# Transposing the residual for five RMS norms: TensorE transposes replaced by VectorE squares and 32-partition DMAs on ScalarE's queue

## The chip, the cores and the metric

The kernel runs on one core of a Trainium2 chip. The metric is the device time of one execution in microseconds. One more execution is taken by the hardware profiler, and its records are the trace that is read here. The engines are called as the profile calls them: PE is TensorE's matmul side and PEld its weight loads, DVE is VectorE, ACT is ScalarE, POOL is GpSimd, and SPq is the queue of SyncE, which issues DMAs.

## The reference

Two decoder layers act on a residual `h` of 256 tokens by 2048 channels in float32. Cut to what matters here:

```python
for i in range(2):
    hn = rms_norm(h, ln_mix_w[i])
    h = h + (even_mixer, odd_mixer)[i](hn, ...)          # ends with  @ w_out  (2048 x 2048)
    hn = rms_norm(h, ln_mlp_w[i])
    h = h + square(relu(hn @ w_up[i])) @ w_down[i]       # 2048 x 8192 and 8192 x 2048
    hn = rms_norm(h, ln_ple_w[i])
    h = h + sigmoid(hn @ w_ple_gate[i]) * (p[i] @ w_ple_proj[i])
return rms_norm(h, ln_final_w)
```

Six of the seven norms feed a matmul, so six times the residual is needed with its channels on the partitions. The last norm only scales rows.

## The kernel before

**Layout.** `h` lies in SBUF as 128 partitions by 2 token tiles by 2048 channels: tokens on the partitions. A matmul with `h` wants the channels on the partitions. So a `Norm` object turns `h` block by block; a block is 512 channels, and a norm has 4 of them. The turned and scaled residual goes into an `XT`: for each group of 128 channels (a k-tile, 16 in all) a high part, rounded to the format `fp32r`, and a low part, the rest. The scale by the root mean square is applied later; `stats` sums the squares of a block on ACT (the operand is called `junk`).

**Weights.** `split_w` loads a chunk (two k-tiles by 512 columns, 512 KB) with a DMA on SP's queue into `wraw` (4 buffers). ACT writes its high part `whi` (L198), then DVE the low part `wlo` (L199); each has 3 buffers. So a chunk costs one ACT cast and one DVE subtraction, and ACT can cast a chunk when PE is done with the chunk three earlier. A product of two float32 numbers is three matmuls: high by high, high by low, low by high.

**Projections.** `project` takes a chunk in 12 matmuls of 512 columns; `project_wide`, which `w_up` and layer 1's input projection use, in 16 matmuls of 512 or 256 columns. Eight chunks make one projection (`nb`) of 512 output columns. At the end of a projection `nb` of `out_proj`, of the last quarter of `w_down`, and of `ple`, `h` gets its new 512 columns, and `close` starts the norm's block for them.

**Order of the work.** A block is a generator. It waits in the lane "tail" of `Background`, and the next projection advances it by one step at each tick, once or twice per chunk. For the last block of a norm `close` drains the lane at once, so all of that block's instructions stand ahead of the next projection in program order. A scheduler may shift instructions a little within an engine. Each engine then works in program order, and an instruction that waits holds up all behind it.

**A block before.** PE transposes 8 squares of 128 x 128 into two PSUM banks (L175); from there ACT writes the high parts (L224) and DVE the low parts (L225), 4 instructions each of 256 columns.

**Semaphores of DMAs.** All DMAs of all queues count on eight semaphores (DMAHW0 to DMAHW7), which are given out in turn. A DMA on a semaphore starts only when the DMA that had it before has landed.

Of the kernel before, what the change touches and what calls it, by code (L numbers as in the profile page):

```python
# [10 lines left out]
F32 = mybir.dt.float32  # L11
# [6 lines left out]
D = 2048  # L18
# [107 lines left out]
def pause(n):  # L126

    for _ in range(n):
        yield
# [3 lines left out]
def trunk_kernel(ctx, tc, a, out):  # L133
# [68 lines left out]
    class XT:  # L202
# [11 lines left out]
        def put(self, k, n, src, scale=None):  # L214
            o = k % 4
            g = self.group(k // 4)
            w, l = g[:, o:o + n, 0, :], g[:, o:o + n, 1, :]
            if len(src.shape) == 2:
                w, l = g[:, o, 0, :], g[:, o, 1, :]
            if scale is None:  # L220
                nc.scalar.copy(out=w, in_=src)
                nc.vector.tensor_tensor(out=l, in0=src, in1=w, op=ALU.subtract)
            else:
                nc.scalar.activation(out=w, in_=src, func=AF.Copy, scale=scale)  # L224
                nc.vector.scalar_tensor_tensor(  # L225
                    out=l, in0=src, scalar=scale, in1=w, op0=ALU.mult, op1=ALU.subtract
                )
# [23 lines left out]
        nc.tensor.matmul(out=ps[t], lhsT=xh, rhs=wl, start=False, stop=False)  # L251
        nc.tensor.matmul(out=ps[t], lhsT=xl, rhs=wh, start=False, stop=last)  # L252

    def project(ps, xt, kts, w, col, ncol=NB, row_of=None):

        n = len(kts)
        for c, m, (wh, wl) in chunks(kts, row_of or list(kts), w, col, ncol):
            for j in range(m):
                for t in range(NT):
                    multiply(ps, xt, kts[c + j], t, wh[:, j, :], wl[:, j, :], c + j == 0, c + j == n - 1)  # L260
                bg.tick(rates)
# [52 lines left out]
    def add_halves(dst, ps, pool):  # L314
        s = pool.tile([P, T], F32, tag="half", name="half", bufs=2)
        nc.scalar.copy(out=s, in_=ps[:, T:2 * T])  # L316
        nc.vector.tensor_add(out=dst, in0=ps[:, 0:T], in1=s)  # L317

    def acc_pair():
        return [atile() for _ in range(NT)]  # L320


    class Norm:


        def __init__(self, which, layer):
            self.which, self.layer = which, layer
            self.xt = XT()
            self.ss = spool.tile([P, NT, 4], F32, tag="ss", name="ss")
            self.cols = None  # L330

        def stats(self, b, ts=range(NT)):
            for t in ts:
# [2 lines left out]
                    out=junk, in_=h[:, t, b * NB:(b + 1) * NB], func=AF.Square, accum_out=self.ss[:, t, b:b + 1]  # L336
                )

        def block(self, b):
            for k in range(4 * b, 4 * b + 4, 2):  # L340
                ps = mtile()
                for j in range(2):
                    for t in range(NT):
                        transpose(ps[:, j * T + t * P:j * T + (t + 1) * P], h[:, t, (k + j) * P:(k + j + 1) * P])
                yield
                for j in range(2):
                    v, c = (vec1, 32 * self.which - 32) if self.which else (vec0, 0)
                    c += 16 * self.layer + k + j
                    self.xt.put(k + j, 1, ps[:, j * T:(j + 1) * T], v[:, c:c + 1])
            yield  # L350
            self.stats(b)
            yield
# [12 lines left out]
    class FinalNorm(Norm):  # L365


        def __init__(self, lnf):
            self.ss = spool.tile([P, NT, 4], F32, tag="ss", name="ss")
            self.lnf = lnf  # L370

        def scale(self, t, b):
            o = h[:, t, b * NB:(b + 1) * NB]
# [65 lines left out]
    def close(norm, b):  # L439

        bg.drain("tail")
        bg.add("tail", norm.block(b))
        if b == 3:
            bg.drain("tail")

    def out_proj(yt, w, kts, norm):
# [9 lines left out]
    def mlp(layer, norm, after):  # L456
        ms = norm.mean_square()
        r2 = spool.tile([P, NT], F32, tag="r2", name="r2")
        nc.vector.reciprocal(out=r2, in_=ms)
        with tc.tile_pool(name="uT", bufs=6) as upool, tc.tile_pool(name="u", bufs=3) as up:  # L460
            for fb in range(4):
                ut = XT(upool)
                for nb in range(4):
                    ps = project_wide(norm.xt, range(KT), a["w_up"][layer], fb * 2048 + nb * NB)
                    for f in range(4):
                        u = up.tile([P, T], F32, tag="u", name="u")
                        add_halves(u, ps[f], up)
# [24 lines left out]
    def ple(layer, norm, after, pT, pp):  # L492
        rs = norm.rstd()
        for nb in range(4):
# [9 lines left out]
            if end:  # L504
                with tc.tile_pool(name="last", bufs=4) as last:
                    project_apart(ps, norm.xt, a["w_ple_gate"][layer], nb * NB, last)
            else:
                project(ps, norm.xt, range(KT), a["w_ple_gate"][layer], nb * NB)
            for t in range(NT):
                g = pp.tile([P, NB], F32, tag="gate", name="gate", bufs=2)  # L510
                nc.scalar.activation(out=g, in_=ps[t], func=AF.Sigmoid, scale=rs[:, t:t + 1])  # L511
# [9 lines left out]
    def even_mixer(norm, after):  # L521
# [3 lines left out]
        with ExitStack() as st:  # L525
# [6 lines left out]
            def first_rows(c):  # L532

                if c % 4 == 0:
                    bg.drain("tail")
                    load_x(c // 4)
                    gen = norm.block(c // 4)
                    for _ in range(3):
                        next(gen)
                    bg.add("stats", gen)  # L540
                    if c == 12:
                        load_vectors()
                        rates["stats"] = 1
# [471 lines left out]
            for blk in range(2):  # L1015
                channels(Z0 + blk * NB, z_tile(blk))
            bg.drain("tail")
            out_proj(yt, a["ev_w_out"][0], list(range(8, 16)) + list(range(8)), after)


    def odd_mixer(norm, after):
        w_in = a["od_w_in"][0]
        xt = norm.xt
        with ExitStack() as st:
# [8 lines left out]
            yt = XT()  # L1033

            def channels(col, dst, then=None):
                ps = project_wide(xt, range(KT), w_in, col)
                bg.drain("tail")
                if not rows:
                    rows[0] = row_rstd(rs, big)
# [124 lines left out]
            for b in range(2):  # L1164
# [9 lines left out]

                channels(5120 + b * NB, gt, finish)
            bg.drain("tail")
            out_proj(yt, a["od_w_out"][0], range(KT), after)


# [39 lines left out]
    for layer in range(2):  # L1219
        mix, after = (even_mixer, odd_mixer)[layer], Norm(1, layer)  # L1220
        mix(norm, after)
        with tc.tile_pool(name="ple", bufs=1) as pp:
            pT = load_p(layer, pp)
            gate = Norm(2, layer)
            mlp(layer, after, gate)
            if layer == 0:
                norm = Norm(0, 1)
            else:
                lnf = pp.tile([P, D], F32, name="lnf")
                nc.sync.dma_start(out=lnf, in_=a["ln_final_w"].rearrange("(o d) -> o d", o=1).to_broadcast([P, D]))  # L1230
                norm = FinalNorm(lnf)
            ple(layer, gate, norm, pT, pp)
# [26 lines left out]
```

## Time and profile before

| | |
|---|---|
| median of 3 runs | 2504.76 us (2504.16 to 2504.85) |
| the profiled execution's own time | 2507.46 us |
| its span, first to last instruction | 2505.7 us |
| granted TensorE clock, mean | 0.998 of full speed |
| PE busy | 2482.6 us, 99% |
| PEld, DVE, ACT busy | 2150.6, 1493.3, 1179.2 us |
| DMA of the one hardware queue | 58.7% of the 16 DMA engines |

The profiled execution is 0.1% longer than the median run. Its span leaves 1.8 us of its own time outside.

### The profile page before, as it was taken

How to read it: one execution, taken by the hardware profiler on the slowest of the kernel's cores; microseconds unless marked ns; L12 is line 12 of the kernel's file. 1: busy time of each engine (PE TensorE's matmuls, PEld its weight loads, DVE VectorE, ACT ScalarE, POOL GpSimd, SP SyncE). 2: the span in 40 equal slices, each digit the busy share in tenths (PEclk: the TensorE clock that was granted, in tenths of full speed). 3: DMA queues.
4: the chain of work that ended last, by engine and by line, in shares of the span. 5: the costliest groups of instructions: out<-in, count | busy, mean ns of one | idle time of the engine just before them, and what ended most of it. 6: DMA issues, size and time to landing. Idle time of an engine off the chain costs nothing. (4 is left out here: it accounts for less than half of the span.)

```text
span 2505.7 us, 34856 instructions
## 1 busy us (share of the span) xinstructions
PE 2482.6 (99%) x13699; PEld 2150.6 (86%) x13699; DVE 1493.3 (60%) x2083; ACT 1179.2 (47%) x1610; POOL 24.2 (1%) x62
## 2 busy tenths in 40 slices
PE   8999999999999999999999999999999999999998
PEld 8999998888888888888888888888888888888886
DVE  5777865565565565565565465656556555556555
ACT  5523664544444443445554453554434444445454
POOL 0000000000000000000000000000000000000000
PEclk9999999999999999999999999999999999999999
DMA  6443456665665665665566655666566566566554
GB/s 206 130 124 107 122 168 191 182 191 189 190 192 189 190 190 192 189 190 182 186 214 191 192 151 168 199 184 192 187 192 190 190 192 189 190 193 187 185 189 153
DMA packets 237125, 452.88 MB, mean 181 GB/s; under 512 B 16417, under 2 KB 19361, under 8 KB 236705
## 3 DMA queue, kind: packets, MB, share of 16 engines
q1 hardware_dynamic: 236960, 450.66, 58.7%
q8 instruction: 107, 1.75, 0.3%
q14 instruction: 58, 0.47, 0.0%
HBM read 448.50 MB, written 2.10 MB: 180 GB/s over the span
## 5 line engine op out<-in xcount | busy, mean ns | idle before, releaser
L199 DVE TENSOR_TENSOR wlo<-wraw,whi 128x1024 fp32r<-128x1024 f32 x840 | 1027.1, 1225 | 899.1 <-ACT whi L198 895.0
L198 ACT CAST whi<-wraw 128x1024 fp32r<-128x1024 f32 x840 | 881.9, 1051 | 1192.6 <-PE acc L252 608.3
L303 PE MATMUL acc<-xt,whi 128*128 128x512 f32 x2560 | 806.1, 396 | 0.0
L250 PE MATMUL acc<-whi,xt 128*128 128x512 f32 x1664 | 655.3, 394 | 0.0
L252 PE MATMUL acc<-whi,xt 128*128 128x512 f32 x1664 | 650.8, 391 | 0.0
L251 PE MATMUL acc<-wlo,xt 128*128 128x512 f32 x1664 | 646.9, 389 | 0.0
L307 PEld LDWEIGHTS acc<-xt,wlo 128*128 128x128 f32 x2560 | 480.7, 188 | 113.4
L307 PE MATMUL acc<-xt,wlo 128*128 128x256 f32 x2560 | 503.5, 278 | 0.0
L303 PEld LDWEIGHTS acc<-xt,whi 128*128 128x128 f32 x2560 | 391.0, 189 | 1.2
L252 PEld LDWEIGHTS acc<-whi,xt 128*128 128x128 f32 x1664 | 312.3, 188 | 70.2
L251 PEld LDWEIGHTS acc<-wlo,xt 128*128 128x128 f32 x1664 | 312.5, 188 | 66.7
L250 PEld LDWEIGHTS acc<-whi,xt 128*128 128x128 f32 x1664 | 312.7, 188 | 62.1
L288 PE MATMUL acc<-xt,whi 128*128 128x256 f32 x768 | 224.2, 294 | 2.3 <-ACT whi L198 1.7
L289 PE MATMUL acc<-xt,whi 128*128 128x256 f32 x768 | 219.1, 286 | 0.8 <-DVE xt L225 0.8
L290 PE MATMUL acc<-xt,wlo 128*128 128x256 f32 x768 | 218.6, 286 | 0.8 <-DVE wlo L199 0.8
L288 PEld LDWEIGHTS acc<-xt,whi 128*128 128x128 f32 x768 | 148.4, 194 | 3.5 <-ACT whi L198 2.6
L289 PEld LDWEIGHTS acc<-xt,whi 128*128 128x128 f32 x768 | 149.1, 194 | 1.3 <-DVE xt L225 1.0
L290 PEld LDWEIGHTS acc<-xt,wlo 128*128 128x128 f32 x768 | 148.3, 194 | 1.5 <-DVE wlo L199 1.4
L316 ACT COPY half<-acc 128x256 f32<-128x256 f32 x160 | 59.1, 370 | 40.6 <-DVE u L317 22.8
L225 DVE SCALAR_TENSOR_TENSOR xt<-mps,vec,xt 128x256 fp32r<-128x256 f32 x96 | 43.2, 479 | 16.3 <-ACT xt L224 16.0
L468 DVE SCALAR_TENSOR_TENSOR u<-u 128x256 f32<-128x256 f32 x128 | 51.0, 419 | 0.3
L317 DVE TENSOR_TENSOR u<-acc,half 128x256 f32<-128x256 f32 x128 | 50.8, 417 | 0.0
(270 smaller groups left out, 1078.6 us busy)
## 6 DMA issues: line engine op xcount, KB each, us to landing
wraw<-in_w_up SPq DMA_DIRECT2D x256, 512.0 KB, 3.7
wraw<-in_w_down SPq DMA_DIRECT2D x256, 512.0 KB, 3.7
wraw<-in_ev_w_in SPq DMA_DIRECT2D x96, 512.0 KB, 4.3
wraw<-in_od_w_in SPq DMA_DIRECT2D x96, 512.0 KB, 3.7
wraw<-in_w_ple_gate SPq DMA_DIRECT2D x64, 512.0 KB, 4.3
wraw<-in_ev_w_out SPq DMA_DIRECT2D x32, 512.0 KB, 4.6
wraw<-in_od_w_out SPq DMA_DIRECT2D x32, 512.0 KB, 4.7
wraw<-in_w_ple_proj SPq DMA_DIRECT2D x8, 512.0 KB, 4.5
```

The lines of the kernel that those rows point to most:

```text
L198: nc.scalar.copy(out=w, in_=r)
L199: nc.vector.tensor_tensor(out=l, in0=r, in1=w, op=ALU.subtract)
L250: nc.tensor.matmul(out=ps[t], lhsT=xh, rhs=wh, start=first, stop=False)
L251: nc.tensor.matmul(out=ps[t], lhsT=xh, rhs=wl, start=False, stop=False)
L252: nc.tensor.matmul(out=ps[t], lhsT=xl, rhs=wh, start=False, stop=last)
L288: nc.tensor.matmul(out=ps[f], lhsT=wh[:, j, s], rhs=xt.hi(k), start=first and f % 2 == 0, stop=False)
L289: nc.tensor.matmul(out=ps[f], lhsT=wh[:, j, s], rhs=xt.lo(k), start=False, stop=False)
L290: nc.tensor.matmul(out=ps[f], lhsT=wl[:, j, s], rhs=xt.hi(k), start=False, stop=last and f % 2 == 1)
L303: nc.tensor.matmul(out=ps[f], lhsT=wh[:, j, s], rhs=xt.both(kts[c + j]), start=c + j == 0, stop=False)
L307: nc.tensor.matmul(out=ps[f][:, 0:T], lhsT=wl[:, j, s], rhs=xt.hi(kts[c + j]), start=False, stop=c + j == n - 1)
L316: nc.scalar.copy(out=s, in_=ps[:, T:2 * T])
L468: nc.vector.scalar_tensor_tensor(out=u, in0=u, scalar=0.0, in1=u, op0=ALU.max, op1=ALU.mult)
```

## The change

All norms but the first (which still uses the old block under the name `block_on_pe`) turn a block in another way, 20 blocks in all:

1. One DVE instruction transposes each 32 x 32 square of the block in place of its partition quarter (L362, 128 x 1024).
2. Sixteen DMAs on ACT's queue (L368) move pieces of 32 partitions by 4 runs of 64 numbers (256 bytes) to the partition quarter where they belong, from the tile `turned` to the tile `placed`.
3. `stats` and a pause of four ticks follow. Then come four `put`s, which read `placed` in SBUF: ACT writes 128 x 256 high numbers (L222); the low part is two DVE instructions of 128 x 128 (L224).
4. For a norm's last block `close` runs the first four steps at once and leaves the rest to the ticks; the new hook `whole` drains the lane before chunk 6 of the next projection.

The two tiles share buffers that exist: of the recurrent part in layer 0's mixer, of a query tile in layer 1's, and of the tile `lnf` in `ple`. So the loads of `lnf`, `pin`, `swab` and `retd` come at other places in SP's queue.

```diff
     class Norm:
+        first_steps = 4
         def block(self, b):
+            turned, placed = self.stage()
+            src = h[:, :, b * NB:(b + 1) * NB].rearrange("p t (j c) -> p j t c", c=S)
+            nc.vector.transpose(out=turned, in_=src)
+            yield
+            sq = turned.rearrange("p (k q t r) -> p k q (t r)", q=SB, t=NT, r=S)
+            to = placed.rearrange("p (k i u) -> p k i u", k=4, i=SB)
+            for i in range(SB):
+                for q in range(SB):
+                    nc.scalar.dma_start(out=to[q * S:(q + 1) * S, :, i], in_=sq[i * S:(i + 1) * S, :, q])
+                if i % 2:
+                    yield
+            self.stats(b)
+            yield
+            yield from pause(4)
+            x = placed.rearrange("p (k i t r) -> p k t i r", k=4, i=SB, t=NT)
+            for j in range(4):
+                k = 4 * b + j
+                self.xt.put(k, 1, x[:, j], self.gain(k))
+                yield
+
+        def block_on_pe(self, b):
             for k in range(4 * b, 4 * b + 4, 2):
                 ps = mtile()
...
     def close(norm, b):
         bg.drain("tail")
-        bg.add("tail", norm.block(b))
+        gen = norm.block(b)
         if b == 3:
+            for _ in range(norm.first_steps):
+                next(gen)
+        bg.add("tail", gen)
+
+    def whole(c):
+        if c == KT - 4:
             bg.drain("tail")
...
-                    ps = project_wide(norm.xt, range(KT), a["w_up"][layer], fb * 2048 + nb * NB)
+                    ps = project_wide(norm.xt, range(KT), a["w_up"][layer], fb * 2048 + nb * NB, whole)
...
-                project(ps, norm.xt, range(KT), a["w_ple_gate"][layer], nb * NB)
+                project(ps, norm.xt, range(KT), a["w_ple_gate"][layer], nb * NB, before=whole)
...
+            after.stage = lambda: [lru_tile(n).rearrange("p a t -> p (a t)") for n in ("rr", "ii")]
             out_proj(yt, a["ev_w_out"][0], list(range(8, 16)) + list(range(8)), after)
```

Where the instructions stand, first ACT, at the end of the third projection (`nb` = 2) of layer 1's `out_proj`. Before, from the last cast ahead of the block (names with their buffer numbers, and in brackets the semaphores that an instruction waits for):

```order
L198 CAST whi_14977<-wraw_14976 128x1024 [waits DMAHW2_49,DVE_49,PE_49]
L335 ACTIVATE junk_14972,ss_11888<-h_77 128x512 [waits DVE_49]
L335 ACTIVATE junk_14974,ss_11888<-h_77 128x512 [waits DVE_49,Activation_49]
L224 ACTIVATE xt_14940<-mps_14929,vec1_79 128x256 [waits PE_49]
L198 CAST whi_14995<-wraw_14994 128x1024 [waits DMAHW3_49,DVE_49,PE_49]
```

And of the change at the same place:

```order
L198 CAST whi_15148<-wraw_15147 128x1024 [waits DMAHW0_49,DVE_49,PE_49]
L349 ACTIVATE junk_15143,ss_12023<-h_77 128x512 [waits DVE_49]
L349 ACTIVATE junk_15145,ss_12023<-h_77 128x512 [waits DVE_49,Activation_49]
L368 DMA stage_15101<-stage_15101 32x4x64 [waits DVE_49]
L368 DMA stage_15101<-stage_15101 32x4x64 x3
L368 DMA stage_15101<-stage_15101 32x4x64 [waits DMAHW1_49]
L368 DMA stage_15101<-stage_15101 32x4x64 [waits DMAHW2_49]
L368 DMA stage_15101<-stage_15101 32x4x64 [waits DMAHW3_49]
L368 DMA stage_15101<-stage_15101 32x4x64 [waits DMAHW4_49]
L368 DMA stage_15101<-stage_15101 32x4x64 [waits DMAHW5_49]
L368 DMA stage_15101<-stage_15101 32x4x64 [waits DMAHW6_49]
```

Six more DMAs like these follow, which wait for DMAHW7 and DMAHW0 to DMAHW4, and then the next cast, `whi_15166`. All sixteen DMAs now stand in one row between two casts, where one activation stood. The first waits for the DVE transpose. The fourth has DMAHW0 and the fifth DMAHW1; DMAHW6 goes first to a weight load that SP issues between the second and the third, that of `wraw_15232`. So the tenth DMA waits for that load.

DVE at the same place, before:

```order
L452 TENSOR_TENSOR h_77<-h_77,acc_14744 128x512 [waits PE_49]
L452 TENSOR_TENSOR h_77<-h_77,acc_14745 128x512 [waits PE_49]
L199 TENSOR_TENSOR wlo_14978<-wraw_14976,whi_14977 128x1024 [waits DMAHW2_49,Activation_49]
L225 SCALAR_TENSOR_TENSOR xt_14940<-mps_14929,vec1_79,xt_14940 128x256 [waits Activation_49]
L199 TENSOR_TENSOR wlo_14996<-wraw_14994,whi_14995 128x1024 [waits DMAHW3_49,DVE_49,Activation_49]
```

And of the change:

```order
L500 TENSOR_TENSOR h_77<-h_77,acc_14905 128x512 [waits PE_49]
L362 STREAM_TRANSPOSE stage_15101<-h_77 128x1024 [waits DVE_49]
L199 TENSOR_TENSOR wlo_15149<-wraw_15147,whi_15148 128x1024 [waits DMAHW0_49,Activation_49]
L199 TENSOR_TENSOR wlo_15167<-wraw_15165,whi_15166 128x1024 [waits DMAHW1_49,Activation_49]
L199 TENSOR_TENSOR wlo_15185<-wraw_15183,whi_15184 128x1024 [waits DMAHW2_49,Activation_49]
```

The transpose stands ahead of the subtraction `wlo_15149`. That subtraction frees the buffer into which SP loads `wraw_15232`, so this load starts after the transpose and the subtraction. The same pattern stands in all 20 blocks: in 19 the tenth DMA waits so, in one block of `ple` the eleventh.

SP at the start of layer 1's MLP, before, with the small loads among those of `od_w_out`:

```order
L197 DMA wraw<-in_od_w_out 128x2x512 x7
L484 DMA pin<-in_p 128x2x256
L197 DMA wraw<-in_od_w_out 128x2x512 x3
L1230 DMA lnf<-in_ln_final_w 128x2048
L197 DMA wraw<-in_od_w_out 128x2x512 x22
```

And of the change:

```order
L197 DMA wraw<-in_od_w_out 128x2x512 x32
L197 DMA wraw<-in_w_up 128x2x512 x9
L532 DMA pin<-in_p 128x2x256
L197 DMA wraw<-in_w_up 128x2x512 x23
```

The load of `pin` now stands behind nine loads of `w_up`; PE's four transposes of it stand at the end of that projection's fifth chunk.

## Rows read from the trace of the kernel before

**Rows 1.** The page's busy time of each engine.

```profile
PE 2482.6 (99%) x13699; PEld 2150.6 (86%) x13699; DVE 1493.3 (60%) x2083; ACT 1179.2 (47%) x1610; POOL 24.2 (1%) x62
```

**Rows 2.** Waits: us in total, times, longest us.

```profile
DVE wlo L199 <- ACT whi L198: 895.0, 673, 3.7
ACT whi L198 <- PE acc L252: 608.3, 387, 1.7
```

**Rows 3.** Timeline of PE, end of the third projection of layer 1's out_proj.

```profile
1660.65 0.39 PE L250 MATMUL acc<-whi,xt 128*128 128x512 f32 x1
```

**Rows 4.** Timeline of ACT at the same place: start, us, engine, line.

```profile
1658.13 1.05 ACT L198 CAST whi<-wraw 128x1024 fp32r<-128x1024 f32 x1 [1.67 <-PE acc L252]
1660.85 1.06 ACT L198 CAST whi<-wraw 128x1024 fp32r<-128x1024 f32 x1 [1.67 <-PE acc L252]
...
1663.10 0.18 ACT L335 ACTIVATION_READ_ACCUMULATOR junk<-h 128x1 f32 x1
```

**Rows 5.** Timeline of DVE at the same place.

```profile
1660.36 1.28 DVE L452 TENSOR_TENSOR h<-h,acc 128x512 f32<-128x512 f32 x2
1661.94 1.23 DVE L199 TENSOR_TENSOR wlo<-wraw,whi 128x1024 fp32r<-128x1024 f32 x1 [0.30 <-ACT whi L198]
```

**Rows 6.** Timeline of PE in a block's first half, w_down of layer 1.

```profile
2328.40 0.39 PE L252 MATMUL acc<-whi,xt 128*128 128x512 f32 x1
2328.63 0.60 PE L175 MATMUL mps<-base,h 128*128 128x128 f32 x4
...
2329.30 0.40 PE L251 MATMUL acc<-wlo,xt 128*128 128x512 f32 x1
```

**Rows 7.** Groups by shape: busy us, mean ns of one.

```profile
L778 DVE STREAM_TRANSPOSE dc<-dct 128x128 f32<-128x128 f32 x16 | 4.3, 296 | 0.0
L965 DVE TENSOR_TENSOR ii<-ii,xc 128x1024 f32<-128x1024 f32 x2 | 2.5, 1226 | 6.8 <-ACT ii L960 6.8
```

**Rows 8.** Timeline of SP's queue, DMAs issued one behind the other.

```profile
1.19 0.41 SPq L1193 DMA_DIRECT2D base<-in_c_base  x1
1.65 0.43 SPq L1194 DMA_DIRECT2D h<-in_x  x1
...
38.37 0.46 SPq L616 DMA_DIRECT2D dtb<-in_dn_dt_bias  x1
38.88 0.42 SPq L617 DMA_DIRECT2D alog<-in_dn_a_log  x1
```

**Rows 9.** Tile r, the shortest DMA issue: ns min/median/max.

```profile
L1206 SPq DMA_DIRECT2D r<-in_lru_bx x1: 272/272/272, 16.2 to 16.2; - x1
```

**Rows 10.** The page's DMA issues: median us from issue to landing.

```profile
wraw<-in_w_down SPq DMA_DIRECT2D x256, 512.0 KB, 3.7
wraw<-in_od_w_out SPq DMA_DIRECT2D x32, 512.0 KB, 4.7
```

**Rows 11.** Tile wraw in the stretch 1640 to 1690: landing of its loads.

```profile
DMA to landing us min/median/max: 3.6/4.7/4.9
```

**Rows 12.** Windows: PE busy, PEld, DVE, ACT, POOL, granted clock, DMA share, GB/s.

```profile
24.00:25.00 1.00, 1.00 (x6) 1.00 (x6) 0.59 (x3) 0.14 (x1) 0.79 (x5) 0.50 0.94 342
...
26.00:28.00 2.00, 2.00 (x17) 2.00 (x17) 0.58 (x1) 1.05 (x1) 0.00 (x0) 0.87 0.70 265
```

**Rows 13.** Timeline of PE in the first 32 us.

```profile
9.56 0.58 PE L288 MATMUL acc<-xt,whi 128*128 128x256 f32 x1 [1.55 <-ACT whi L198]
...
15.84 0.41 PE L290 MATMUL acc<-xt,wlo 128*128 128x256 f32 x1
...
17.00 0.28 PE L289 MATMUL acc<-xt,whi 128*128 128x256 f32 x1
...
22.90 0.41 PE L289 MATMUL acc<-xt,whi 128*128 128x256 f32 x1 [0.78 <-DVE xt L225]
```

**Rows 14.** The page's DMA queue: packets, MB, share of 16 engines.

```profile
q1 hardware_dynamic: 236960, 450.66, 58.7%
```

More of the change, by code (lines that the diff above doesn't have):

```diff
@@ L219, in put @@
                 w, l = g[:, o, 0, :], g[:, o, 1, :]
+            elif scale is not None:
+                w, l = (g[:, o, v].rearrange("p (t i r) -> p t i r", t=NT, i=SB) for v in range(2))
+                nc.scalar.activation(out=w, in_=src, func=AF.Copy, scale=scale)
+                for t in range(NT):
+                    nc.vector.scalar_tensor_tensor(
+                        out=l[:, t], in0=src[:, t], scalar=scale, in1=w[:, t], op0=ALU.mult, op1=ALU.subtract
+                    )
+                return
             if scale is None:
@@ L252, in multiply, with project @@
         nc.tensor.matmul(out=ps[t], lhsT=xl, rhs=wh, start=False, stop=last)
-    def project(ps, xt, kts, w, col, ncol=NB, row_of=None):
+    def project(ps, xt, kts, w, col, ncol=NB, row_of=None, before=None):
         n = len(kts)
-        for c, m, (wh, wl) in chunks(kts, row_of or list(kts), w, col, ncol):
+        for c, m, (wh, wl) in chunks(kts, row_of or list(kts), w, col, ncol, before):
             for j in range(m):
@@ L317, in add_halves, with halves_of @@
         nc.vector.tensor_add(out=dst, in0=ps[:, 0:T], in1=s)
+    def halves_of(tile_):
+        both = tile_()
+        return both[:, 0:NT * NB], both[:, NT * NB:]
     def acc_pair():
@@ L323, in trunk_kernel, with __init__ @@
     class Norm:
-        def __init__(self, which, layer):
-            self.which, self.layer = which, layer
+        first_steps = 4
+        def __init__(self, which, layer, stage=None):
+            self.which, self.layer, self.stage = which, layer, stage
             self.xt = XT()
@@ L337, in stats, with gain @@
                 )
+        def gain(self, k):
+            v, c = (vec1, 32 * self.which - 32) if self.which else (vec0, 0)
+            c += 16 * self.layer + k
+            return v[:, c:c + 1]
         def block(self, b):
+            turned, placed = self.stage()
[18 more added lines that the diff above has]
+        def block_on_pe(self, b):
             for k in range(4 * b, 4 * b + 4, 2):
@@ L346, in block @@
                 for j in range(2):
-                    v, c = (vec1, 32 * self.which - 32) if self.which else (vec0, 0)
-                    c += 16 * self.layer + k + j
-                    self.xt.put(k + j, 1, ps[:, j * T:(j + 1) * T], v[:, c:c + 1])
+                    self.xt.put(k + j, 1, ps[:, j * T:(j + 1) * T], self.gain(k + j))
             yield
@@ L370, in __init__ @@
             self.lnf = lnf
+        first_steps = 0
         def scale(self, t, b):
@@ L536, in first_rows @@
                     load_x(c // 4)
-                    gen = norm.block(c // 4)
+                    gen = norm.block_on_pe(c // 4)
                     for _ in range(3):
@@ L1035, in channels @@
             def channels(col, dst, then=None):
-                ps = project_wide(xt, range(KT), w_in, col)
+                ps = project_wide(xt, range(KT), w_in, col, whole if not rows else None)
                 bg.drain("tail")
@@ L1176, in odd_mixer @@
             bg.drain("tail")
+            after.stage = lambda: halves_of(
+                lambda: big.tile([P, 8, T], F32, tag="cqT", name="stage").rearrange("p k t -> p (k t)")
+            )
             out_proj(yt, a["od_w_out"][0], range(KT), after)
@@ L1223, in trunk_kernel @@
             pT = load_p(layer, pp)
-            gate = Norm(2, layer)
+            stage = lambda: halves_of(lambda: pp.tile([P, D], F32, tag="lnf", name="stage"))
+            gate = Norm(2, layer, stage)
             mlp(layer, after, gate)
             if layer == 0:
-                norm = Norm(0, 1)
+                norm = Norm(0, 1, stage)
             else:
-                lnf = pp.tile([P, D], F32, name="lnf")
+                lnf = pp.tile([P, D], F32, tag="lnf", name="lnf")
                 nc.sync.dma_start(out=lnf, in_=a["ln_final_w"].rearrange("(o d) -> o d", o=1).to_broadcast([P, D]))
```

## The prediction

> **What bounds the kernel now.** I read the page's busy times first: PE is busy for 2482.6 of 2505.7 us [rows 1], so a microsecond less on PE is a microsecond of the end, and any stall of PE is one too. DVE at 60% and ACT at 47% have room on the mean, but a mean does not show how far ahead of PE they are at one place. The list of waits shows that: DVE's largest wait is for ACT's casts, and ACT's is for PE, 387 times and never over 1.7 us there [rows 2]. So the weights go ACT, DVE, PE, and ACT starts a cast only when PE gives a buffer back. The lead is three chunks and no more.
>
> Next I took the timeline at one block, the end of the third projection of layer 1's `out_proj`. PE begins the fourth at 1660.65 [rows 3]. The cast that this release allows starts at 1660.85, and casts stand 2.72 us apart, which is a chunk's time on PE [rows 4]. At 1660.65 PE thus holds two ready chunks and a third that is being cast: it can run without further casts for 3 x 2.72 us, to 1668.8. It then needs the next chunk's high part at once and its low part after one matmul of 0.23 us (the start distance in [rows 6]), at 1669.0. Cast and subtraction take 1.05 and 1.23 us one behind the other [rows 4, 5], 2.3 us with the step between. **So the next cast must start by 1666.7**, or PE stands.
>
> **What is removed.** In the timeline of PE, four transposes stand between two matmuls: from the matmul ahead of them to the second matmul behind them it is 0.90 us, where two distances of 0.23 would be 0.46 [rows 6]. Four cost 0.44 us. 20 blocks of eight make 160 transposes: **-17.6 us**. ACT's and DVE's evictions from PSUM are replaced by as many ACT writes and twice as many shorter DVE ones; both engines have idle time beside PE, so I put these at nothing. Without that cover they would be bounded by a few tenths of a microsecond per block on DVE.
>
> **What is added to DVE.** One transpose of 128 x 1024. The trace has it at 128 x 128 only, 296 ns. An elementwise instruction of 128 x 1024 takes 1226 ns [rows 7]; eight times 296 would be 2.37. I take 1.23, as the other instructions there have a fixed part too. It stands ahead of the subtraction of the chunk just cast. The adds to `h` end at 1661.64 [rows 5], the transpose at 1662.87, the subtraction at 1664.1.
>
> **What is added to ACT.** Sixteen DMA issues in one row. The trace shows no DMA on ACT, only on SP: starts 0.46 to 0.51 us apart when nothing is waited for [rows 8], the shortest single issue 0.272 us [rows 9]. I take 0.46, the distance of most of them. ACT's squares end at 1663.3 [rows 4], so without other waits sixteen issues last until 1670.6, already 3.9 us beyond the deadline.
>
> The Trainium skill (DMA: Bandwidth & Descriptors, section "Issuing engines are not separate DMA queues") says that the time to issue a DMA is usually small relative to the DMA itself. For one DMA here this holds (0.46 against a landing of 3.7); if sixteen together were small too, their term would be 0, and only the wait of the next paragraph would be left.
>
> **The wait that the change adds.** DMAs share eight semaphores, and the order shows that the tenth of a block waits for a weight load that SP issues in between, which itself waits for the subtraction that the transpose put back. That load is issued at 1664.1 and lands 4.7 us later (median of `od_w_out`; 3.7 for `w_down` [rows 10]; 3.6 to 4.9 about this place [rows 11]): 1668.8. Nine issues are over by 1667.4, so ACT stands until 1668.8, and seven more issues take it to 1672.0. Behind them the next cast ends at 1673.1 and its subtraction at 1674.35. PE needed it at 1669.0: **a stall of 5.3 us**. With 3.7 for the landing it is 4.3. There are six non-last blocks of `out_proj` and six of `w_down`; the other eight (last blocks, and `ple`, where two casts or copies stand differently) I put at the mean, 4.8. **20 x 4.8 = +96 us.**
>
> The puts behind it wait for the sixteenth DMA. By then PE has two chunks again, and the puts add less than 2 us to ACT, so I add nothing; if the DMAs land late, this is where it shows. `pin` now lands after PE reaches its transposes: 0 to about 4 us, once; I take 0.
>
> **The clock.** After PE stood for 0.78 us in the start-up, matmuls resumed at 22.90 [rows 13]; the granted clock was 0.50 (the level of 1.2 GHz) at 24 to 25 and 0.87 on the mean from 26 to 28, so it rose to 2.4 GHz at about 26.5 [rows 12]. That is 3.6 us at half speed, 1.8 lost. After the wait of 1.55 us that ended at 9.56, single matmuls of 256 columns show as 0.41 us still at 15.84 and as 0.28 at 17.00 [rows 13]: some 6.5 us, 3.2 lost. A stall of 4 to 5 us is longer than both waits. I take the middle, 2.5 us for each block: **+50 us**.
>
> **Sum.** 96 + 50 - 17.6 = +128 us. On the profiled execution's 2507.5 that is 2636; that execution is 2.7 us above the median of the runs, so I forecast **2633 us**. Bounds: with 0.272 for an issue and 3.6 for the landing the stall is 2.9 us, with 1.8 for the clock the sum +76, 2581 us. With 0.51, 4.9 and 3.2 it is 5.9 us and +163, and with the longest transpose 23 more: 2691 us.
>
> **Rivals.**
>
> *Only the issues count* (chance 0.12): the load lands before the ninth issue is over. Then the stall is 1670.6 + 2.3 - 1669.0 = 3.9 us, the sum 78 + 50 - 17.6 = +110: 2615 us. For it: landing times vary by over 1 us. Against it: the load cannot start before 1664.1, and no landing in this stretch is under 3.6.
>
> *The clock stays up* (0.14): 96 - 17.6 = +78, 2583 us. For it: the two places where it fell are both in the start-up, where PE had just begun. Against it: the second fell after a wait of under 1 us.
>
> *The small packets clog the DMA engines* (0.10): a block adds 2048 packets of 256 bytes. The trace's packets, mostly of 2 KB, cost 0.587 x 16 x 2505.7 / 236960 = 99 ns of an engine each [rows 14]. If a small one cost as much, the nine DMAs around the load would add 72 packets, 7.1 us, to each engine's queue before it lands; by their bytes it would be 0.9. Half of 7.1 puts 3.5 us on each block: 2703 us. The Trainium skill (DMA: Bandwidth & Descriptors, section "Why small descriptors are slow (HBM only)") says that transfers from SBUF to SBUF do not suffer from small descriptors; no run here shows it yet, and by it this rival would fall away.
>
> *PE keeps its lead* (0.04): faster by the transposes alone, 2504.8 - 17.6 = 2487 us. It decides at 1666.7: from the end of the squares that leaves 3.4 us, so the sixteen issues must take 0.21 us or less each, and the tenth's load must land within 2.6 us. Both are below the shortest row. It would come true if a DMA issue did not hold up ACT's next instruction and the semaphore's wait did not either.
>
> **How the numbers follow.** The forecast itself has 0.60, its own range 2581 to 2691. I give 2570 to 2695: it takes in the two rivals at 2583 and 2615 and leaves out the clogged engines, the faster case, and some tails of the forecast, together near 0.2. Within 0.2% (5 us, about what a measurement of this kernel can tell from no change) the gain and the loss would have to cancel, a stall under 1 us in each block: 0.02. Faster 0.04, slower 0.94.
>
> **What would show each step.** In the profile after: ACT's sixteen DMA issues in one row with starts 0.4 to 0.5 us apart, and a gap of over 1 us ahead of the tenth; the cast behind them starting some 11 us after PE's new projection, not 3; PE idle 20 times for 4 to 5 us with the cast or the subtraction as its releaser; granted clock 0.5 for some microseconds behind each; L175 with 32 transposes of `h` instead of 192. The forecast is wrong if issues on ACT take a tenth of SP's time, if no gap stands at the tenth DMA, or if the clock stays at 1.0 in the chunk behind a stall.

## The result, and the profile after

The changed kernel takes 2661.2 us (median of 4 runs, 2660.6 to 2662.0); before took 2504.6 on the same chip (4 runs). The ratio is 1.0626, with a 95% interval of 1.0607 to 1.0644: slower by 156.5 us, where 128 was forecast. The time lies in the range given.

The page of the profile after: busy time, the granted clock in 40 slices, the queue of the new DMAs (packets, MB, share of 16 engines), and their issues with KB each and median us to landing.

```profile
PE 2521.0 (95%) x13539; PEld 2164.6 (81%) x13539; DVE 1520.9 (57%) x2183; ACT 1178.3 (44%) x1610; POOL 24.2 (1%) x62
PEclk9999998899999999998889999989999999999899
q10 hardware_dynamic: 46080, 10.51, 2.2%
stage<-stage ACTq DMA_DIRECT2D x256, 32.0 KB, 1.9
```

The line of issues counts 256 of the 320 DMAs; the 64 of layer 0's four `out_proj` blocks stand under the names of the shared buffers there, `ii<-rr`. PE has 160 instructions fewer than in [rows 1] and is "busy" for 38 us more, since its matmuls run longer where the clock is down; 5% of the span it stands. ACT's busy time is what it was, because issuing is not counted as busy. A reader who goes by busy shares alone finds nothing on ACT.

The list of waits shows it (us in total, times, longest):

```profile
ACT whi L198 <- DMA stage<-stage: 146.5, 14, 11.4
PE acc L258 <- ACT whi L198: 98.2, 17, 6.9
PE acc L311 <- ACT whi L198: 16.4, 3, 5.7
PEld acc L259 <- DVE wlo L199: 12.9, 17, 0.8
```

PE's waits for casts are new: 17 and 3 make the 20 blocks, 114.6 us in all. ACT's first row names a DMA as the releaser. The timeline of ACT below corrects that. The new lines of the kernel (ns minimum, median, maximum; then issue to landing in us):

```profile
L362 DVE STREAM_TRANSPOSE stage<-h x16: 1236/1245/1248, 1158.7 to 2542.2; 128x1024 f32<-128x1024 f32 x16
L368 ACTq DMA_DIRECT2D stage<-stage x256: 592/612/1539, 1159.9 to 2553.2; - x128
DMA to landing us min/median/max: 1.9/1.9/5.0
```

The timeline of ACT at the end of the third projection of layer 1's `out_proj`, the place of [rows 4] (start, length, and in brackets the idle time ahead with its releaser):

```profile
1766.43 1.05 ACT L198 CAST whi<-wraw 128x1024 fp32r<-128x1024 f32 x1 [1.67 <-PE acc L260]
...
1768.14 0.63 ACT L349 ACTIVATE junk<-h 128x512 bf16<-128x512 f32 x1
1768.53 0.59 ACTq L368 DMA_DIRECT2D stage<-stage  x1
...
1769.45 9.91 ACTq L368 DMA_DIRECT2D stage<-stage  x15
1779.40 1.99 ACT L198 CAST whi<-wraw 128x1024 fp32r<-128x1024 f32 x2 [10.54 <-DMA stage<-stage]
```

The "wait for a DMA" of 10.54 us is ACT's own queue: 15 issues in 9.91 us, 0.66 each, and the cast starts 0.04 us behind the last. In all 20 blocks ACT's next instruction starts 0.04 us behind the last issue. The view of waits does not count the issues as ACT's work, so it puts the gap down to the event nearest to its end.

PE at the same place, in the timeline and in windows (us, PE, PEld, DVE, ACT and POOL busy, granted clock, DMA share, GB/s):

```profile
1766.23 0.39 PE L258 MATMUL acc<-whi,xt 128*128 128x512 f32 x1
...
1774.17 0.39 PE L260 MATMUL acc<-whi,xt 128*128 128x512 f32 x1
1780.50 1.22 PE L258 MATMUL acc<-whi,xt 128*128 128x512 f32 x2 [5.95 <-ACT whi L198]
1781.76 0.80 PE L259 MATMUL acc<-wlo,xt 128*128 128x512 f32 x1
...
1782.78 0.63 PE L259 MATMUL acc<-wlo,xt 128*128 128x512 f32 x1
1783.21 0.63 PE L260 MATMUL acc<-whi,xt 128*128 128x512 f32 x1
...
1786.09 0.39 PE L258 MATMUL acc<-whi,xt 128*128 128x512 f32 x1
```

```profile
1778.00:1780.00 2.00, 0.00 (x0) 0.00 (x0) 0.00 (x0) 0.60 (x1) 0.00 (x0) 0.79 0.29 49
1780.00:1782.00 2.00, 1.46 (x3) 0.74 (x4) 1.52 (x2) 2.00 (x4) 0.00 (x0) 0.50 0.10 16
1784.00:1786.00 2.00, 2.00 (x6) 1.55 (x5) 2.00 (x5) 0.00 (x0) 0.00 (x0) 0.51 0.94 340
1786.00:1788.00 2.00, 2.00 (x10) 1.65 (x10) 0.70 (x2) 1.05 (x1) 0.00 (x0) 1.00 0.92 288
```

PE's new projection begins at 1766.23. PE runs dry three chunks later, at 1774.40 (0.23 behind the last start), and starts again at 1780.50, when the cast is done. The two matmuls with the high part take 1.26 us to the next start; at 1.2 GHz (0.43 us from start to start, against 0.23) they would take 0.86, so I count 0.4 as the wait for the low part, which the list of waits shows only on PEld. The granted clock falls while PE stands, between 1778 and 1780, and is 0.50, the level of 1.2 GHz, until 1786. That is twelve matmuls with 0.2 us more each: 2.4 us.

### The profile page after: what moved, and what is told of

It is laid out like the page before. It is cut to its first block, busy times and chain, and to the rows that moved or that the text cites. A ratio compares the mean times of both kernels' runs of the same rounds, so it can differ in the third digit from the quotient of the medians.

```text
span 2659.0 us, 35059 instructions
## 1 busy us (share of the span) xinstructions
PE 2521.0 (95%) x13539; PEld 2164.6 (81%) x13539; DVE 1520.9 (57%) x2183; ACT 1178.3 (44%) x1610; POOL 24.2 (1%) x62
## 3 DMA queue, kind: packets, MB, share of 16 engines
q10 hardware_dynamic: 46080, 10.51, 2.2%
## 5 line engine op out<-in xcount | busy, mean ns | idle before, releaser
L258 PE MATMUL acc<-whi,xt 128*128 128x512 f32 x1664 | 668.0, 404 | 98.2 <-ACT whi L198 98.2
L259 PE MATMUL acc<-wlo,xt 128*128 128x512 f32 x1664 | 666.8, 401 | 0.7
L260 PE MATMUL acc<-whi,xt 128*128 128x512 f32 x1664 | 663.4, 399 | 0.0
L258 PEld LDWEIGHTS acc<-whi,xt 128*128 128x128 f32 x1664 | 320.8, 194 | 171.9 <-ACT whi L198 105.2
L259 PEld LDWEIGHTS acc<-wlo,xt 128*128 128x128 f32 x1664 | 321.8, 193 | 81.7 <-DVE wlo L199 12.9
L260 PEld LDWEIGHTS acc<-whi,xt 128*128 128x128 f32 x1664 | 321.7, 193 | 71.6
L230 DVE TENSOR_TENSOR xt<-u,xt 128x256 fp32r<-128x256 f32 x128 | 50.2, 418 | 0.0
```

The lines of the kernel that those rows point to most:

```text
L258: nc.tensor.matmul(out=ps[t], lhsT=xh, rhs=wh, start=first, stop=False)
```

## The experiments

The loss against the run without DMAs (E1) is used below as a yardstick: 174 us in the changed kernel, 8.7 per block.

**E1, no DMAs.**

```diff
-                    nc.scalar.dma_start(out=to[q * S:(q + 1) * S, :, i], in_=sq[i * S:(i + 1) * S, :, q])
...
-            x = placed.rearrange("p (k i t r) -> p k t i r", k=4, i=SB, t=NT)
+            x = turned.rearrange("p (k i t r) -> p k t i r", k=4, i=SB, t=NT)
```

> Leaves out the sixteen DMAs of a block; the puts read the tile that VectorE wrote, so the squares stay in their partition quarters. The VectorE transposes, the split puts and the moved loads all stay. Theory A (PE stands because sixteen DMA issues in a row hold ScalarE for 10.4 us, and loses more at the lower clock behind each stall): with the issues gone ScalarE's cast is in time, PE never stands in a block, and what is left is the removal of 160 transposes: 2504.6 - 17.6 = 2487 us, 2480 to 2495, granted clock 0.998 again. Rival B (VectorE's transpose of 1.25 us and the doubled short low parts make the subtractions late): 20 stalls of about a microsecond stay, 2505 us or more. Rival C (the moved loads of pin, swab and retd cost): 2490 to 2500, at one place each.

Measured: 2487.0 us (2485.6 to 2488.5), ratio 0.9928 (0.9913 to 0.9943), granted clock 0.999. The page's busy row:

```profile
PE 2460.5 (99%) x13539; PEld 2133.0 (86%) x13539; DVE 1522.5 (61%) x2183; ACT 1180.5 (48%) x1610; POOL 24.3 (1%) x62
```

The forecast to the microsecond: 17.9 us gained (before took 2505.0 beside it), 17.6 worked out. If the 17.6 is right, VectorE's transpose, the split puts and the moved loads together cost nothing on the path; rivals B and C fall. All of the loss hangs on the DMAs.

**E2, four issues.**

```diff
             for i in range(SB):
-                for q in range(SB):
-                    nc.scalar.dma_start(out=to[q * S:(q + 1) * S, :, i], in_=sq[i * S:(i + 1) * S, :, q])
+                nc.scalar.dma_start(out=to[:, :, i], in_=sq[:, :, i])
```

> Four DMAs of 128 partitions in place of sixteen of 32: the same bytes and the same 2048 packets of 256 bytes per block, but the squares are not moved to another partition quarter (left out). It tells the number of issues from what they carry. Theory A with a fixed price per issue (0.655 us from start to start): ScalarE is held for 2.7 us instead of 10.4, its next cast starts some 5 us after PE's new projection, just under the 6.05 that PE's lead allows: no stall, 2487 us, at most 2500. Theory A with a price that grows with the descriptors of a DMA (4.9 ns for each run of 256 bytes): four issues take four times 2.5 us, as long as sixteen, 2640 to 2665 us. Rival D (the packets, not the issues, cost the time): about 2660 too, but with short issues in the trace and long landings.

Measured: 2490.0 us (2489.4 to 2492.5), ratio 0.9943 (0.9927 to 0.9960). The DMA line of this run, with the landing:

```profile
L367 ACTq DMA_DIRECT2D stage<-stage x64: 601/662/917, 1126.7 to 2381.8; - x64
DMA to landing us min/median/max: 2.3/4.4/7.4
```

An issue that carries four times as much costs 0.662 in place of 0.612 us. The price is one per issue, hardly one by the partition, the run or the byte. The runs of 256 bytes (rival D) are as many as in the changed kernel (42240 packets on the queue against 46080), and what they cost is at most the 3 us to E1: landings are longer here, and PE hardly notices.

**E7 and E10, eight and twelve issues.** The row's length between four and sixteen:

```diff
+                for half in (slice(0, 64), slice(64, P)):
+                    nc.scalar.dma_start(out=to[half, :, i], in_=sq[half, :, i])
...
+                for part in (slice(0, 32), slice(32, 64), slice(64, P)):
+                    nc.scalar.dma_start(out=to[part, :, i], in_=sq[part, :, i])
```

> Eight DMAs of 64 partitions in place of sixteen of 32, same bytes and packets, on ScalarE's queue; the squares are not moved to another partition quarter (left out). By theory A the row lasts 8 times 0.655 = 5.2 us, the cast behind it ends 8.95 us after PE's new projection began and PE has run dry at 8.16: a wait of 0.8 us for the high part and 0.75 for the low part, 31 us in all, against 5.7 and 0.75 with sixteen. It also tells what the clock costs behind a short stall: if the clock falls only behind long ones, 2487 + 31 = 2518 us; if each stall of a microsecond costs the same 2.2 us as now, 2562. With no link between the row's length and the stall: 2490 or 2660.

> Twelve DMAs (per quarter of the free dimension one of 64 partitions and two of 32) in place of sixteen of 32, on ScalarE's queue, same bytes and packets; the squares are not moved to another partition quarter (left out). It stands between eight issues, where each block lost 1.75 us and the granted clock stayed at 1.00, and sixteen, where it lost 8.7 with the clock. By theory A the row grows by 4 times 0.655 = 2.6 us over that of eight: 4.4 us per block, 2574 us, if the clock does not fall behind a stall of that length, and 2618 us with the 2.2 us per block that it costs behind the long ones. Were the loss not linear in the row's length (a wait that sets in with some DMA of the row): 2522 or 2661.

Measured: eight 2521.6 us (2519.7 to 2523.0), ratio 1.0066 (1.0053 to 1.0080); twelve 2606.3 us (2604.6 to 2606.9), ratio 1.0399 (1.0382 to 1.0416). Against E1 a block loses 0.15 us with four issues, 1.7 with eight, 6.0 with twelve and 8.7 with sixteen. From twelve to sixteen it is 2.7 us, the four issues. From eight to twelve it is 4.2: the four issues and 1.6 us more. PE's timeline and windows at one block of E7, then of E10:

```profile
1138.40 0.74 PE L258 MATMUL acc<-whi,xt 128*128 128x512 f32 x2 [0.44 <-ACT whi L198]
1139.66 0.50 PE L259 MATMUL acc<-wlo,xt 128*128 128x512 f32 x1 [0.52 <-DVE wlo L199]
```

```profile
1139.00:1140.00 1.00, 0.48 (x2) 0.30 (x2) 1.00 (x2) 1.00 (x3) 0.00 (x0) 1.00 0.00 0
1140.00:1141.00 1.00, 1.00 (x6) 0.83 (x5) 1.00 (x3) 1.00 (x3) 0.00 (x0) 1.00 0.09 23
```

```profile
1187.00 0.73 PE L258 MATMUL acc<-whi,xt 128*128 128x512 f32 x2 [2.98 <-ACT whi L198]
1188.26 0.79 PE L259 MATMUL acc<-wlo,xt 128*128 128x512 f32 x1 [0.53 <-DVE wlo L199]
```

```profile
1188.00:1190.00 2.00, 1.74 (x4) 1.45 (x5) 2.00 (x5) 2.00 (x5) 0.00 (x0) 0.55 0.34 80
1190.00:1192.00 2.00, 2.00 (x7) 1.53 (x7) 2.00 (x6) 0.45 (x2) 0.00 (x0) 0.60 0.97 323
1192.00:1194.00 2.00, 2.00 (x10) 1.65 (x9) 1.10 (x4) 1.05 (x1) 0.00 (x0) 1.00 0.89 287
```

With eight issues PE waits 0.44 and 0.52 us in the block shown and the clock stays at 1.00, as in all 20 blocks; in the one with the longest wait it is 1.47 and 0.53. With twelve it waits 2.98 and 0.53 in the block shown and the clock falls to half for about 3 us; it falls in all 20. So the loss has the two parts that the prediction gave it, and the clock's part sets in between. The expectation for twelve named 2574 without the clock's part and 2618 with the whole of it; it is nearer to the second.

**E3, SyncE's queue.**

```diff
-                    nc.scalar.dma_start(out=to[q * S:(q + 1) * S, :, i], in_=sq[i * S:(i + 1) * S, :, q])
+                    nc.sync.dma_start(out=to[q * S:(q + 1) * S, :, i], in_=sq[i * S:(i + 1) * S, :, q])
```

> The same sixteen DMAs, issued on SyncE's queue, where the weight loads stand, in place of ScalarE's. Theory A: ScalarE is free, so its casts go on at once. SyncE is held for 16 times 0.46 to 0.66 us, 7.4 to 10.5 us, in which no weight load is issued. A load has 9.6 us from its issue to the cast that needs it and lands in 4.6, 5.0 to spare, and the cast may be 5.85 us late itself, together 10.9: so PE just keeps its lead, 2487 us, at most 2520 where a wait for a landing adds to SyncE's row. Rival E (the price is the DMAs' landing or their shared semaphores, whichever engine issues): the puts and casts wait as before, 2600 us or more. If SyncE issues these in 0.46 us and ScalarE in 0.655, the price of an issue depends on the engine; if both take 0.655, on the DMA's shape.

Measured: 2562.0 us (2558.5 to 2564.6), ratio 1.0226 (1.0211 to 1.0242). A miss for both: ACT's casts behind the squares are in time, as Theory A said, but 75 us remain. The issue's length on SP, and the timeline of ACT at the third block of layer 0's `w_down`:

```profile
L368 SPq DMA_DIRECT2D stage<-stage x256: 585/599/1563, 1139.5 to 2457.0; - x128
```

```profile
1201.04 1.70 ACT L222 ACTIVATE xt<-stage,vec 128x256 fp32r<-128x256 f32 x4 [6.52 <-DMA stage<-stage]
1203.91 1.04 ACT L198 CAST whi<-wraw 128x1024 fp32r<-128x1024 f32 x1 [1.17 <-DMA wraw<-in_w_down]
```

The `put`s stand behind three casts in ACT's program. There they now wait for the last DMA, which SP issues only at about 1199, and the next cast waits behind them, and then for a weight load that SP issued late. PE waits 3.33 us at 1205.01. The wait has moved from the issues to the puts. An issue on SP takes 0.599 us, so ACT is not what makes it dear.

**E4, GpSimd's queue** (the same line with `nc.gpsimd`).

> The same sixteen DMAs, issued on GpSimd's queue, which is nearly idle and holds no other DMA. Theory A: neither ScalarE nor the weight loads stand behind an issue. If GpSimd issues one in 0.66 us or less, the last lands 13 us after the transpose, about when the puts are due, and the time is 2487 us, 2480 to 2500. If an issue takes GpSimd 1.3 us or more, the row takes over 21 us, the puts wait on ScalarE with the casts behind them, and the stalls come back later in the projection: 2600 us or more. No run so far shows a DMA issued by GpSimd. Rival E (landing and semaphores): 2600 us or more in either case, with short issues.

Measured: 2502.7 us (2498.9 to 2504.9), ratio 0.9989 (0.9979 to 0.9998): within 0.2% of before. The issue on GpSimd, its landing, and the put with the longest wait, in ACT's timeline:

```profile
L368 POOL DMA_DIRECT2D stage<-stage x256: 548/548/583, 1130.4 to 2402.6; - x128
DMA to landing us min/median/max: 1.7/4.4/7.1
```

```profile
1314.40 1.70 ACT L222 ACTIVATE xt<-stage,vec 128x256 fp32r<-128x256 f32 x4 [3.51 <-DMA stage<-stage]
```

The expectation's 2480 to 2500 is missed by 2.7 us. In sixteen of the twenty blocks PE does not wait. In the other four, all last blocks of a norm, it waits up to 3.0 us (in the block shown), 8.7 us in all, and the clock falls to 0.50 behind the longest. The put shown starts 16 us behind its block's transpose at 1298.44, and the last block's numbers are needed for the last quarter of the very next projection. The waits are 8.7 of the 15.7 us that this run lacks to E1, and the clock behind the longest adds to them; the rest is not accounted for.

**E5, one long run per partition.**

```diff
-            src = h[:, :, b * NB:(b + 1) * NB].rearrange("p t (j c) -> p j t c", c=S)
-            nc.vector.transpose(out=turned, in_=src)
+            for q in range(SB):
+                src = h[:, :, b * NB:(b + 1) * NB].rearrange("p t (k q c) -> p q k t c", q=SB, c=S)[:, q]
+                nc.vector.transpose(out=turned[:, q * T:(q + 1) * T], in_=src)
...
+                    nc.scalar.dma_start(out=to[q * S:(q + 1) * S, i], in_=sq[i * S:(i + 1) * S, q])
```

> The whole computation, with the squares laid out so that each DMA moves one run of 1 KB per partition in place of four runs of 256 bytes; VectorE's transpose becomes four of 128 x 256, at most 0.5 us more per block. Still sixteen issues in a row on ScalarE. What sets the price of an issue? If it is a fixed price of this kind of transfer, 0.655 us from start to start: 2661 us as before, 2650 to 2672. If it is the access pattern (a weight load, one issue of SyncE of 0.37 us, has long runs), some 0.41 us: the row takes 6.6 us, the stall falls by 3.9 us in each of 20 blocks to about 2 and 0.75 behind it, 2565 to 2590 us.

Measured: 2652.9 us (2651.5 to 2655.0), ratio 1.0593 (1.0577 to 1.0610); an issue takes 0.602 us in the median. A quarter of the runs changes the price by a hundredth of a microsecond: the fixed price holds, and the access pattern falls. The run is 8.3 us faster than the change; a row lasts 10.14 us in most blocks in place of 10.38, which is 5 of them.

**E9, from HBM.**

```diff
-                    nc.scalar.dma_start(out=to[q * S:(q + 1) * S, i], in_=sq[i * S:(i + 1) * S, q])
+                    nc.scalar.dma_start(out=to[q * S:(q + 1) * S, i], in_=a["w_up"][0][i * S:(i + 1) * S, q * T:(q + 1) * T])
```

> Sixteen DMAs per block on ScalarE's queue with the shape of the run with one long run (32 partitions by 1 KB), but read from a weight in HBM in place of the turned tile; the squares are left out of the result. They wait for nothing of the block, so they stand spread among the casts, and only the length of an issue is read from this run, no time. Theory G (a transfer whose both ends are in SBUF is dear to issue): 0.37 to 0.47 us, like the loads and the stores of SyncE, against 0.60. Theory H (ScalarE's queue, or small transfers of 32 partitions, are dear): 0.60 again.

This kernel ran once, and its time is not used. The line of its issues:

```profile
L368 ACTq DMA_DIRECT2D stage<-in_w_up x256: 317/396/1447, 400.8 to 2369.9; - x128
```

The same queue and the same shape, read from HBM: 0.396 us against 0.602. Theory G holds and H falls: ACT issues as fast as SP in [rows 8], and what is dear is a transfer with both ends in SBUF. A source in SBUF alone is not: the eight stores of `out` from SBUF to HBM in the trace before took SP 0.400 us in the median. Nor is the step to another partition quarter: E2's issues leave it out and take 0.662. That the issues stand apart here is not the reason either: in E8 they do too, and take 0.612.

**E8, spread over the ticks.**

```diff
-        first_steps = 4
+        first_steps = 2
...
+            self.stats(b)
             for i in range(SB):
                 for q in range(SB):
                     nc.scalar.dma_start(out=to[q * S:(q + 1) * S, :, i], in_=sq[i * S:(i + 1) * S, :, q])
-                if i % 2:
-                    yield
-            self.stats(b)
-            yield
-            yield from pause(4)
+                    if i < 2 or q % 2:
+                        yield
```

> The whole computation, all sixteen issues still on ScalarE, but handed out over the ticks, so that five or six stand ahead of the next cast and two to four between the later ones. Theory A with PE's lead (what counts is how late a cast is, and not how long ScalarE issues in all): each cast is in time or up to half a microsecond late, and only the last blocks of a norm, whose puts now wait for a DMA issued some 15 us after the projection began, lose 2 to 5 us each: 2490 to 2520 us. Rival F (the total of 10.4 us of issues per block counts, wherever it stands): about 2660.

Measured: 2514.0 us (2510.4 to 2515.2), ratio 1.0033 (1.0021 to 1.0045). ACT's timeline in a block of layer 1's `out_proj`:

```profile
1644.89 5.05 ACTq L369 DMA_DIRECT2D stage<-stage  x7
1649.99 1.05 ACT L198 CAST whi<-wraw 128x1024 fp32r<-128x1024 f32 x1 [5.03 <-DMA stage<-stage]
```

All sixteen issues still stand on ACT and take as long each (0.612 us in the median); 147 of the 174 us are gone. The cast shown is held up for 5 us, and PE does not wait for it. Rival F falls: what counts is how long a cast is held up, against PE's lead, not how much ACT issues. Of the 27 us that are left, PE's list of waits shows 18: 6.2 for low parts, 6.9 for casts and 5.0 for puts.

**E6, three queues.** Six on GpSimd, six on SyncE, four on ScalarE:

```diff
+            queue = dict(G=nc.gpsimd, S=nc.sync, A=nc.scalar)
             for i in range(SB):
                 for q in range(SB):
-                    nc.scalar.dma_start(out=to[q * S:(q + 1) * S, :, i], in_=sq[i * S:(i + 1) * S, :, q])
+                    e = queue["GSAGSGSAGSAGSGSA"[SB * i + q]]
+                    e.dma_start(out=to[q * S:(q + 1) * S, :, i], in_=sq[i * S:(i + 1) * S, :, q])
```

> The whole computation, the sixteen DMAs of a block dealt out to three queues: six on GpSimd, six on SyncE, four on ScalarE. Theory A (a row of issues costs only by what stands behind it on its own queue): ScalarE's four end before the cast is due, as in the run with four; SyncE's six take 3.9 us of the 5.0 that a weight load has to spare; GpSimd's six end some 7 us after the block's projection is over and land 4.4 us later, 11.2 us, where the puts wait 2 us and end at 13.0, before the fourth cast is due at 14.2. No stall: 2487 us, 2483 to 2495, faster than both kernels. If the puts' wait makes the fourth cast late in the blocks, as the last blocks did with GpSimd alone, up to 2503. If landings or traffic are the cost: 2600 us or more.

Measured: 2488.1 us (2486.3 to 2490.4), ratio 0.9934 (0.9921 to 0.9946), 0.7% faster than before and 6.5% faster than the change, and within 1.1 us of the run with no DMAs at all. ACT's timeline at one block:

```profile
1645.71 0.61 ACTq L370 DMA_DIRECT2D stage<-stage  x1
...
1646.35 2.19 ACTq L370 DMA_DIRECT2D stage<-stage  x3
1648.58 2.00 ACT L198 CAST whi<-wraw 128x1024 fp32r<-128x1024 f32 x2 [2.54 <-DMA wraw<-in_od_w_out]
...
1652.73 1.70 ACT L222 ACTIVATE xt<-stage,vec 128x256 fp32r<-128x256 f32 x4
```

The puts don't wait here; in two of the twenty blocks they do, 4.6 us in all. The Trainium skill (Perfetto Trace Analysis, section "DMA Optimizations") says that where the writing of descriptors is the bottleneck, an engine full of DMA slices and not the data, dealing the DMAs out over sync, scalar and GPSIMD may help; this run agrees, by 173 us.

## Why the prediction was right, and where its sum was off

The time lies in the range, and the way in which it is lost is the one foreseen: a row of issues holds up the next cast, PE runs dry, and the clock falls behind the wait. One part of the mechanism did not happen, the wait ahead of the tenth DMA, and the prediction had named the lack of a gap there as a sign of being wrong. By its other signs the issues are longer than it said: their starts stand 0.65 apart and not 0.4 to 0.5, the cast starts 13.2 us after PE's new projection (in the block shown) and not some 11, and PE waits 5.2 to 6.9 us and not 4 to 5.

**The transposes, -17.6 us: right.** E1 gives -17.9 with everything else of the change but the DMAs in place. PE has 32 transposes of `h` left where 192 were.

**VectorE's transpose, 1.23 us: right** (1.245). The prediction had it on the path only through the load that the tenth DMA waits for; that wait did not come, and without the DMAs it costs nothing (E1).

**The issue on ACT, 0.46 us: this is the term that was mis-sized.** The step said that the trace shows no DMA on ACT, only on SP, and took SP's distance. The engine was not the difference (E9 on ACT: 0.396; E3 on SP: 0.599). The rows of SP show loads from HBM; the change issues transfers from SBUF to SBUF, of which the trace before has none. These stand 0.65 us apart. Sixteen last 10.4 us in most blocks, not 7.4. The error is one of kind: the nearest row was chosen by operation, and both ends of the transfer should have been compared. My upper bound, 0.51, was the largest of the same rows and so no bound for another kind.

The Trainium skill (DMA: Bandwidth & Descriptors, section "Issuing engines are not separate DMA queues") calls the issue time usually small relative to the DMA. In the changed kernel one issue is 0.61 against a landing of 1.9 us, a third, and the row lasts over five times a landing. The prediction was right not to follow it.

**The wait of the tenth DMA, 1.4 us: did not come.** In the block shown the tenth starts at 1774.84, 0.63 behind the ninth, with no gap. The weight load that it shares its semaphore with is issued when the subtraction ends, at 1769.64, and lands 4.81 us later, at 1774.45, ahead of the ninth issue's end at 1774.80: it had time, just because the issues are slower. In no block does the tenth stand more than 0.1 us behind the ninth's end; in one block of `ple` the eighth waits 1.1 us for the landing of an earlier weight load. What is left is 0.2 us ahead of the ninth: in the chain of work it follows the landing of the second DMA of the row, which lasted 4.73.

```profile
1769.45 4.73 DMA stage<-stage
1774.21 0.59 ACTq L368
...
1774.84 0.61 ACTq L368
```

Here the rival *only the issues count* describes what happened, though not its time: it had the issues too short as well. The two errors, 3.0 us too little for the issues and 1.4 too much for the wait, partly cancel; that the sum came within 28 us is in part luck.

**The stall, 4.8 us per block: 6.3.** The list of waits has 114.6 us for the high part, 5.7 per block; the modelled end of the last matmul ahead hides 0.16 (it is shown 0.39 long, and the next would start 0.23 behind its start), and the low part adds 0.4. 20 x 6.3 = 126 in place of 96. That is the 30 us by which the sum was short.

**The clock, 2.5 us per block: right in size, with luck.** What is left of the loss is 174 - 126 = 48 us, 2.4 per block, as counted in the timeline of one block. It was the shakiest step, a middle between two places of the start-up [rows 12, 13], and neither place is what the prediction took it for:

```profile
6.05 1.97 PE L175 MATMUL mps<-base,h 128*128 128x128 f32 x8 [2.58 <-DMA h<-in_x]
19.04 1.03 PE L175 MATMUL mps<-base,h 128*128 128x128 f32 x8
21.62 0.50 PE L288 MATMUL acc<-xt,whi 128*128 128x256 f32 x2 [0.49 <-ACT xt L224]
```

At 9.56 the pace did not fall behind the wait of 1.55 us: the eight transposes ahead of it, at 6.05, already take 1.97 us where eight take 1.03 at 19.04. And the wait of 0.78 that ended at 22.90 had one of 0.49 shortly ahead of it. The two together are shorter than the 1.47 and 0.53 us behind which E7 has the clock at 1.00, so these waits alone do not tell when it falls. The rival *the clock stays up* is false for sixteen issues and true for eight.

**The puts, nothing: right in the changed kernel**, where ACT issues the DMAs itself and comes to the puts late. E3 and E4 show the place that the prediction named, "if the DMAs land late": there ACT waits 99 and 18 us for landings ahead of the puts.

**The small packets** (rival): 2.2% of 16 engines' span of 2659 us for 46080 packets is 20 ns of an engine each on the mean, not 99. **PE keeps its lead**: false for this change, and true as soon as the issues are dealt out (E6).

126 + 48 - 18 = 156, as measured; the 48 is a remainder here. Counted instead from the starts of PE's matmuls in all 20 blocks, PE stands 118 us for the high parts and loses 57 more behind them against its full pace, the low parts' 8 among these: 175 in all, 49 of it for the clock.

## What to carry to other kernels

A DMA costs the engine that issues it time of its own, and here hardly by what it moves: 0.60 to 0.66 us from SBUF to SBUF on ScalarE, for 32 or 128 partitions and runs of 256 bytes or 1 KB. Multiply it by the number of DMAs in one row, and set that against the lead of whoever waits for the engine's next instruction; then deal the issues out over queues, or put the waiting engine's work between them, before changing the data path. Price an issue from a row of the same kind, with the same ends (HBM or SBUF). And when a wait is moved, look at the consumer of the transfer as well: it stands in an engine's program order like the issue did.

## What was not expected of the hardware

- An issue with both ends in SBUF took 0.60 us on SyncE, 0.61 on ScalarE and 0.55 on GpSimd; with one end in HBM 0.40 (E9; the stores of `out`) and 0.27 to 0.46 [rows 8, 9]. Four times the partitions made it 0.66, a quarter of the runs 0.60. Why the ends matter, these runs don't show.
- Behind a wait of 0.44 and one of 0.52 us, 0.74 us of matmuls apart, the granted clock stayed at 1.00 (E7), and behind 1.47 and 0.53 too. Behind one of 2.98 and one of 0.53 it fell to half (E10), and in the start-up of the kernel before behind 0.49 and 0.78. What makes the difference, these runs don't show.
- The landing of the same 32 KB took, in the median, 1.9 us from ScalarE's row of sixteen and 3.9 from the same sixteen spread (E8), 4.4 from GpSimd's row of sixteen (E4) and 2.2 from GpSimd's six (E6). Why, these runs don't show.
